# A hybrid diffusion backbone on one core: two buffers each for the pooling mixer's inputs and gates, and the modulation's gates stored as rows

## The chip, the cores and the metric

The kernel runs on one core of a Trainium2 chip. The metric is the device time of one execution in microseconds (us), lower is better. Five engines work side by side, each through its own queue in order: PE (TensorE, products; PEld is its weight load), DVE (VectorE), ACT (ScalarE), POOL (GpSimd) and SP (SyncE, which here only issues transfers). Transfers between the chip's DRAM and the on-chip memory run on 16 DMA engines; in this kernel SP issues the weight loads and POOL most others.

## The reference

Two layers work on 512 latent tokens and 256 context tokens, each 1024 wide. Cut to what matters:

```python
for l in range(DEPTH):                                  # DEPTH = 2
    mod   = silu(c)     @ mod_w[l] + mod_b[l]           # 3 x 1024: shift, scale, gate (latents)
    mod_c = silu(c_ctx) @ mod_w[l] + mod_b[l]           # the same for the context
    z, zc = (rmsnorm(x) * (1 + scale) + shift) @ w_in, ...     # one projection for all branches
    y_mla  = attention(...) * silu(z.mla_gate)          # 8 heads, keys of context and latents
    y_pool = (pooled @ pool_w) * pool_scale * silu(z.pool_gate)
    y_gla  = gated_linear_attention(...) * silu(z.gla_gate)
    merged = sum(sigmoid(z.merge_b) * (y_b @ w_branch_b) for b in (mla, pool, gla))
    x  = x  + gate   * rmsnorm(merged @ w_out)
    xc = xc + gate_c * rmsnorm(merged_c @ w_out)        # not in the last layer
```

In the pooling mixer, `pooled` is, for each of four groups of 128 channels, the mean over a window of 2, 4, 8 or 16 tokens minus the token itself.

## The kernel before

All tokens of a layer (768, or 512 where only latents count) lie along the free dimension, channels on the 128 partitions. Products are made in float32 as three products of split halves: each weight load `raw_...` is split by ACT (`wh_...`, line 77) and DVE (`wl_...`, line 78) before PE can use it (`mm3`, lines 91 to 94). What one stage leaves for a later one goes through DRAM.

The kernel is written for a planner. It traces the program once, and when the context closes it orders each engine's instructions by a simulation of the time line (line 1244); the order of the program is the priority, and `urgent` raises it. Buffers are named by tags: tiles of one tag share `bufs` slots, and a tile that takes a slot waits until all users of the slot's former tile are done.

A layer runs in this order: the gated linear attention (`gla_tile`, six token tiles), the projections of the gates and inputs that go to DRAM (`gate_block` for `gg`, `px`, `pg`, `mg`), the output of the linear attention, the **pooling mixer** (lines 689 to 736), the softmax attention (head by head), the 24 merge gates `m1`, `m2`, `m0` (`zA_m` in the profile), the three branch products (`br_p`, `br_g`, `br_m`), and the output product with the residual (`wo`). The planner lays the merge gates, which need only the layer's input, between the steps of the mixer and of the attention.

**The pooling mixer.** A loop over the four groups makes these steps: clear the padded input `u` (POOL, line 700), load it from DRAM (line 702), build the window sums `pn` (DVE, lines 705 to 715), the difference `pv` with its edges (lines 716 to 723), split it (`pvh`, `pvl`), load the gate `sg` (`psg` in the profile, line 728), apply tanh and the gate, multiply by the group's weights (`pps`), put both together in `sg` (line 735) and store it as `yp` (line 736). The mixer takes its buffers from tags that the linear attention used: `u` from `up0`, `sg` from `afab`, each one slot, so that all four groups use the same slot in turn. The tag `e` held the decays of the linear attention (1024 numbers per partition; `u` has 816 or 544), and `lmask` a table of masks (768 numbers; `sg` has 768).

**The modulation.** The 3072 outputs of a layer are made in 12 chunks of 256 (`modulation`, lines 155 to 255). `columns` (line 168) writes a chunk as two columns of `cols`, one channel per partition, for each of two streams (latents and context; one stream for the gates of the last layer). Chunks 8 to 11 are the gates: they are multiplied by the post norm and stored to `grow` in DRAM (lines 178 to 180), one DMA per chunk and stream. At the end of the layer `gate_rows` (line 259) loads each stream's 1024 gates from `grow`, spread over all partitions, as `pg`, which line 1056 and line 1072 multiply by. The chunks are made one after another by `chunk_beside_pe`, on DVE and POOL (`macc`) with a small product `modt` on PE, while the merge gates run: the generator `todo_mod` is advanced at line 913 and line 1000.

Of the kernel before, what the change touches and what calls it, by code (L numbers as in the profile page):

```python
# [11 lines left out]
F32 = mybir.dt.float32  # L12
# [6 lines left out]
P = 128  # L19
D = 1024  # L20
KD = 8
CTX = 256
LAT = 512
T = CTX + LAT
NT = T // P
DEPTH = 2
# [22 lines left out]
def hybrid_kernel(ctx, tc, io, out):  # L49
    nc = tc.nc  # L50
    V, S, G, PE = nc.vector, nc.scalar, nc.gpsimd, nc.tensor
# [8 lines left out]
    stage = ctx.enter_context(tc.tile_pool(name="stage", bufs=2))  # L60
    small = ctx.enter_context(tc.tile_pool(name="small", bufs=4))
    dram = ctx.enter_context(tc.tile_pool(name="dram", bufs=1, space=MemoryType.DRAM))
    psz = ctx.enter_context(tc.tile_pool(name="psz", bufs=2, space=MemoryType.PSUM))
# [3 lines left out]
    def act(out, in_, func=AF.Copy, **kw):  # L67
        return S.activation(out=out, in_=in_, func=func, **kw)  # L68

    def tt(out, a, b, op=ALU.mult, eng=None):  # L70
        return (eng or V).tensor_tensor(out=out, in0=a, in1=b, op=op)  # L71

    def stt(out, a, s, b, op0=ALU.mult, op1=ALU.mult):
        return V.scalar_tensor_tensor(out=out, in0=a, scalar=s, in1=b, op0=op0, op1=op1)  # L74
# [13 lines left out]
    def mm(out, lhsT, rhs, start, stop):  # L88
        PE.matmul(out=out, lhsT=lhsT, rhs=rhs, start=start, stop=stop)  # L89
# [14 lines left out]
    def load_raw(src, nk, width, name, pool=stream):  # L104
        raw = pool.tile([P, nk, width], F32, tag="raw", name=f"raw_{name}", bufs=3 if pool is stream else None)
        nc.sync.dma_start(out=raw, in_=src)
        return raw
# [17 lines left out]
    ident = const.tile([P, P], F32, name="ident")  # L125
# [29 lines left out]
    def modulation(l, pool=None):  # L155


        cols = const.tile([P, 24, 2], F32, tag=f"mcols{l}", name=f"mcols{l}")
        grow = dram.tile([2, D], F32, name=f"grow{l}")
        mods[l] = (cols, grow)  # L160
        modb = small.tile([P, 24], F32, tag="modb", name=f"modb{l}", bufs=1)
        nc.gpsimd.dma_start(out=modb, in_=io["mod_b"][l])
        pre = small.tile([P, KD], F32, tag="pre", name=f"pre{l}", bufs=1)
        nc.gpsimd.dma_start(out=pre, in_=io["pre_norm"][l])
        post = small.tile([P, KD], F32, tag="post", name=f"post{l}", bufs=1)
        nc.gpsimd.dma_start(out=post, in_=io["post_norm"][l])

        def columns(j, pt, streams=2):

            at = slice(2 * j, 2 * j + 2)  # L170
            dst = cols[:, at, 0:streams]

            def spread(v, c0):
                return v[:, 2 * j - c0:2 * j - c0 + 2].unsqueeze(2).to_broadcast([P, 2, streams])

            tt(dst, pt[:, :, 0:streams], spread(modb, 0), ALU.add)
            if j >= 8:
                tt(dst, dst, spread(post, 16))
                for st in range(streams):
                    nc.gpsimd.dma_start(out=grow[st].rearrange("(b p) -> p b", p=P)[:, 2 * j - 16:2 * j - 14], in_=dst[:, :, st])  # L180
            elif j >= 4:

                stt(dst, dst, 1.0, spread(pre, 8), ALU.add, ALU.mult)

        def chunk_on_pe(j):
            parts = j in (5, 6, 3, 7)
            ps = pst.tile([4 if parts else 2, 256], F32, tag="t", name=f"modps{l}_{j}")
            for half in range(2):
                raw = pool.tile([P, 4, 256], F32, tag="raw", name=f"raw_mod{l}_{j}_{half}", bufs=10)
                nc.sync.dma_start(out=raw, in_=io["mod_w"][l, j][:, 4 * half:4 * half + 4, :])  # L190
                if parts:
                    wh = pool.tile([P, 4, 256], F32R, tag="xin", name=f"mwh{l}_{j}_{half}", bufs=6)
                    wl = pool.tile([P, 4, 256], F32R, tag="xin", name=f"mwl{l}_{j}_{half}", bufs=6)
                    act(wh, raw)
                    tt(wl, raw, wh.bitcast(F32), ALU.subtract)
                for k in range(4):
                    kk = 4 * half + k
                    if parts:
                        mm(ps, chl[:, kk, :], wh[:, k, :], kk == 0, False)
                        mm(ps[0:2], chl[:, kk, 0:2], wl[:, k, :], False, kk == KD - 1)  # L200
                    else:
                        mm(ps, csil[:, kk, :], raw[:, k, :], kk == 0, kk == KD - 1)
            n = 4 if parts else 2
            row = pool.tile([n, 256], F32, tag="modrow", name=f"modrow{l}_{j}")
            act(row, ps)
            pt = psz.tile([P, 2, 2], F32, tag="z", name=f"modt{l}_{j}")
            for i in range(2):
                mm(pt[:, i], row[:, i * P:(i + 1) * P], sel[0:n], True, True)
            columns(j, pt)

        def chunk_beside_pe(j):

            streams = 2 if j < 8 or l < DEPTH - 1 else 1
            acc = small.tile([P, 2, 256], F32, tag="macc", name=f"macc{l}_{j}", bufs=1)
            for half in range(2):
                raw = load_raw(io["mod_w"][l, j][:, 4 * half:4 * half + 4, :], 4, 256, f"mod{l}_{j}_{half}")
                for k in range(4):
                    kk = 4 * half + k
                    for st in range(streams):
                        c = csil[:, kk, st:st + 1]  # L220
                        w, a = raw[:, k], acc[:, st]
                        eng = (G if streams == 1 and kk%2 else V) if st==0 else (G if kk%2 else V)
                        if kk == 0:
                            (eng if eng is G else V).tensor_scalar(out=a, in0=w, scalar1=c, scalar2=None, op0=ALU.mult)
                        elif eng is V:
                            stt(a, w, c, a, ALU.mult, ALU.add)
                        else:
                            if eng is S:
                                act(w, w, scale=c)
                            else:  # L230
                                G.tensor_scalar(out=w, in0=w, scalar1=c, scalar2=None, op0=ALU.mult)  # L231
                            tt(a, a, w, ALU.add, G)
            yield
            pt = psz.tile([P, 2, 2], F32, tag="z", name=f"modt{l}_{j}")
            for i in range(2):
                for st in range(streams):
                    mm(pt[:, i, st:st + 1], acc[:, st, i * P:(i + 1) * P], ones, True, True)
            columns(j, pt, streams)


        pend = []
        for j in (0, 4, 1, 5, 2, 6, 3, 7, 8, 9, 10, 11):
            if pool is not None and j < 8:
                chunk_on_pe(j)
            else:
                pend.append(chunk_beside_pe(j))
                next(pend[-1])
                if len(pend) > 1:
                    next(pend.pop(0), None)
            if j == 11 or (pool is None and j == 7):  # L250
                yield
                for chunk in pend:
                    next(chunk, None)
                pend = []
            yield

    mods = {}

    def gate_rows(l, pool, streams):

        grow = mods[l][1]
        res = []
        for s in range(streams):
            pgt = pool.tile([P, D], F32, tag=f"pg{s}", name=f"pg{l}_{s}", bufs=1)
            nc.gpsimd.dma_start(out=pgt, in_=grow[s].partition_broadcast(P))
            res.append(pgt)
        return res

# [81 lines left out]
    def layer(l, hT, close_hT, side, todo_mod):  # L350
# [64 lines left out]
        gl = g1.enter_context(opened(f"gla{l}", 2, side))  # L415
        psg = g1.enter_context(opened(f"psg{l}", 4, None, MemoryType.PSUM))
# [53 lines left out]
        afab = gl.tile([98, T], F32R, tag="afab", name=f"afab{l}", bufs=1)  # L470
# [11 lines left out]
        lmask = gl.tile([P, len(LEVELS), P], U32, tag="lmask", name=f"lmask{l}", bufs=1)  # L482
        nc.gpsimd.dma_start(out=lmask, in_=io["lmask"])

        f, b = slice(0, 64), slice(64, 128)
# [210 lines left out]
        segs = [(16, 0, CTX), (16 + CTX + 16, CTX, LAT)] if full else [(16, CTX, LAT)]  # L696
        W = segs[-1][0] + LAT + 16
        for g, w in enumerate(WINDOWS):
            u = gl.tile([P, W], F32, tag="up0", name=f"pu{l}_{g}", bufs=1)
            G.memset(u, 0.0)  # L700
            for s0, t0, n in segs:
                nc.gpsimd.dma_start(out=u[:, s0:s0 + n], in_=px_d[g][:, t0:t0 + n])
# [21 lines left out]
            pvh = gl.tile([P, T], F32R, tag="up1", name=f"pvh{l}_{g}", bufs=1)  # L724
            pvl = gl.tile([P, T], F32R, tag="dn1", name=f"pvl{l}_{g}", bufs=1)
            split(pvh[:, lo:T], pvl[:, lo:T], pv[:, lo:T])
            sg = gl.tile([P, T], F32, tag="afab", name=f"psg{l}_{g}", bufs=1)
            nc.gpsimd.dma_start(out=sg[:, lo:T], in_=sg_d["p"][g][:, lo:T])
            sig = gl.tile([P, T], F32, tag="pqk", name=f"psig{l}_{g}")
            half_tanh(sig[:, lo:T], sg[:, lo:T])  # L730
# [158 lines left out]
        for i in range(-AHEAD, len(units)):  # L889
            if i + AHEAD < len(units):  # L890
                u = units[i + AHEAD]
# [4 lines left out]
            if i >= 0:  # L896
                u = units[i]
# [358 lines left out]
```

## Time and profile before

| | |
|---|---|
| runs | 1512.39, 1515.74, 1519.95 us; median 1515.74 |
| the profiled execution | 1514.81 us, its span in the profile 1513.0 |
| PE | 1444.7 us busy, 95% of the span |
| DVE, ACT, POOL | 71%, 47%, 34% |
| mean granted clock of PE | 0.984 |
| DMA | 209.75 MB, mean 139 GB/s |

The rows of the profile name an engine, a line of the kernel, and the tiles written and read (out<-in). Where a helper issues an operation its line is the helper's: L89 is every product, L68 every activation, L71 and L74 the two tensor operations of DVE and POOL. In a timeline the first two numbers are the start and the length in us, and the brackets at the end give the idle time of that engine just before and what released it. In the chain of work that ended last, a row with DMA stands for the time from a transfer's issue to its landing. A row of the busy windows gives the stretch, its length, the busy us of PE, PEld, DVE, ACT and POOL with the count of instructions of each, the granted clock of PE, the mean busy share of the DMA engines and what they moved. That share is summed from the packets' own times, so it can pass 1.

### The profile page before, as it was taken

The page shows a single profiled execution, that of the slowest core. Times are in us where ns is not written, and L with a number is a line of the kernel's source. Part 1 is how long each engine was busy: PE and PEld are TensorE (multiplying, and loading weights), DVE is VectorE, ACT ScalarE, POOL GpSimd, SP SyncE. Part 2 cuts the span into 40 slices and gives each one's busy share as a digit, 9 for nine tenths or more (in the row PEclk, how much of TensorE's full clock was granted, in tenths as well). Part 3 has the DMA queues.
Part 4 walks back from the last instruction along what each step waited for, and adds up shares of the span by engine and source line. Part 5 has one row for each costly group of instructions (what it writes and reads, how often), then busy time and mean ns, then how long its engine had stood idle before and what let it go on. Part 6 is the DMA issues. An engine that isn't in the chain of part 4 may idle for free.

```text
span 1513.0 us, 23911 instructions
## 1 busy us (share of the span) xinstructions
PE 1444.7 (95%) x8940; PEld 1279.7 (85%) x8940; DVE 1066.7 (71%) x1980; ACT 717.3 (47%) x1340; POOL 521.8 (34%) x695
## 2 busy tenths in 40 slices
PE   7999999999997999997999999999999999998988
PEld 4799899998886889886879988988988888886778
DVE  3645999757576788876676373789976676686783
ACT  6554453343334445666443345654253555454532
POOL 3432333444243443542111064414463100053550
PEclk9999999999998999998999999999999999999999
DMA  9333323256544532346565234334356523157731
GB/s 366 108 125 113 107 96 115 90 166 192 183 74 101 144 118 90 130 147 163 173 210 198 82 126 129 124 127 127 100 180 204 164 96 96 51 151 145 232 132 69
DMA packets 64195, 209.75 MB, mean 139 GB/s; under 512 B 12464, under 2 KB 15696, under 8 KB 64080
## 3 DMA queue, kind: packets, MB, share of 16 engines
q1 hardware_dynamic: 38688, 116.74, 25.2%
q0 software_dynamic: 24528, 88.34, 18.3%
q10 hardware_dynamic: 864, 3.15, 0.5%
q8 instruction: 70, 1.15, 0.3%
q14 instruction: 45, 0.37, 0.1%
HBM read 161.65 MB, written 46.54 MB: 138 GB/s over the span
## 4 chain that ended last, share of the span: by engine, by line
PE 63%; issue 11%; DVE 11%; DMA 8%; POOL 3%; ACT 3%; POOLq 0%; DVEq 0%; SPq 0%; ACTq 0%
PE zA_m L89 13%; PE zB_gv L89 5%; PE zA_px L89 4%; PE zA_mg L89 4%; PE zB_wo L89 4%; PE wo L89 3%; DMA raw_m<-in_w_in 3%; PE lv L89 3%; PE zA_pg L89 3%; PE zA_gk L89 2%; PE br_p L89 2%; PE br_m L89 2%; PE br_g L89 2%; PE zB_qkv L89 2%; PE zA_gq L89 2%
## 5 line engine op out<-in xcount | busy, mean ns | idle before, releaser
L89 PE MATMUL zA_m<-hh,wh_m 128*128 128x512 f32 (+1 forms) x576 | 206.6, 359 | 1.0 <-ACT wh_m L68 1.0
L89 PE MATMUL zA_m<-hh,wl_m 128*128 128x512 f32 (+1 forms) x576 | 206.7, 359 | 0.6 <-DVE wl_m L71 0.6
L89 PE MATMUL zA_m<-hl,wh_m 128*128 128x512 f32 (+1 forms) x576 | 206.5, 359 | 0.0
L89 PEld LDWEIGHTS zA_m<-hh,wh_m 128*128 128x128 f32 x576 | 110.1, 191 | 16.0 <-ACT wh_m L68 1.4
L89 PEld LDWEIGHTS zA_m<-hh,wl_m 128*128 128x128 f32 x576 | 109.9, 191 | 15.6 <-DVE wl_m L71 1.1
L89 PEld LDWEIGHTS zA_m<-hl,wh_m 128*128 128x128 f32 x576 | 109.9, 191 | 14.4
L68 ACT ACTIVATE wh_m<-raw_m 128x1024 fp32r<-128x1024 f32 x48 | 50.9, 1060 | 93.0 <-PE zA_m L89 45.5
L68 ACT ACTIVATE pe<-sc,mx 128x768 f32<-128x768 f32 (+1 forms) x80 | 65.2, 814 | 60.2 <-DVE mx L831 59.7
L831 DVE TENSOR_REDUCE mx<-sc 128x1 f32<-128x768 f32 (+1 forms) x80 | 67.7, 846 | 34.7 <-PE sc L89 34.0
L71 DVE TENSOR_TENSOR wl_m<-raw_m,wh_m 128x1024 fp32r<-128x1024 f32 x48 | 59.0, 1228 | 45.6 <-ACT wh_m L68 45.1
L231 POOL TENSOR_SCALAR raw_mod<-raw_mod,csil 128x256 f32<-128x256 f32 x64 | 69.2, 1085 | 62.0 <-DVE macc L74 38.5
L74 DVE SCALAR_TENSOR_TENSOR macc<-raw_mod,csil,macc 128x256 f32<-128x256 f32 x132 | 70.8, 547 | 12.4 <-POOL macc L71 10.5
L68 ACT ACTIVATE pth<-pt 128x256 fp32r<-128x256 f32 (+1 forms) x144 | 61.8, 471 | 34.6 <-PE pt L853 34.0
L71 DVE TENSOR_TENSOR ptl<-pt,pth 128x256 fp32r<-128x256 f32 (+1 forms) x144 | 72.6, 534 | 7.2 <-ACT pth L68 6.2
L89 PEld LDWEIGHTS lv<-pqk 128*128 128x128 f32 x560 | 70.8, 191 | 4.7 <-issue 1.8
L347 POOL DMA_DIRECT2D sm<-st_m x32 | 17.6, 550 | 165.5 <-ACT st_m L68 148.1
L89 PE MATMUL lv<-pqk 128*128 128x128 f32 x560 | 73.4, 275 | 1.3 <-DVE pqk L71 1.2
L89 PE MATMUL sc<-kth,qth 96*128 96x256 f32 (+1 forms) x144 | 50.8, 353 | 19.0 <-ACT pe L68 18.9
L71 POOL TENSOR_TENSOR macc<-macc,raw_mod 128x256 f32<-128x256 f32 x64 | 55.1, 860 | 36.4 <-DVE macc L74 30.6
L89 PE MATMUL br_p<-yp,wh_wbp 128*128 128x512 f32 (+1 forms) x192 | 56.3, 376 | 8.6 <-ACT yp L68 6.8
L853 PE MATMUL pt<-ident,pe 128*128 128x128 f32 x416 | 61.3, 273 | 0.7 <-ACT pe L68 0.7
L89 PE MATMUL zB_gv<-wh_gv,hh 128*128 128x256 f32 x192 | 55.7, 291 | 4.1 <-ACT st_gv L68 2.1
(402 smaller groups left out, 4732.8 us busy)
## 6 DMA issues: line engine op xcount, KB each, us to landing
raw_mod<-in_mod_w SPq DMA_DIRECT2D x48, 512.0 KB, 5.0
raw_m<-in_w_in SPq DMA_DIRECT2D x48, 512.0 KB, 3.8
sm<-st_m POOLq DMA_DIRECT2D x24, 384.0 KB, 2.9
raw_wo<-in_w_out SPq DMA_DIRECT2D x16, 512.0 KB, 4.0
sm<-st_m POOLq DMA_DIRECT2D x24, 256.0 KB, 2.5
raw_gv<-in_w_gv SPq DMA_DIRECT2D x8, 512.0 KB, 4.6
raw_gg<-in_w_in SPq DMA_DIRECT2D x8, 512.0 KB, 4.0
raw_px<-in_w_in SPq DMA_DIRECT2D x8, 512.0 KB, 3.7
```

The lines of the kernel that those rows point to most:

```text
L68: return S.activation(out=out, in_=in_, func=func, **kw)
L71: return (eng or V).tensor_tensor(out=out, in0=a, in1=b, op=op)
L74: return V.scalar_tensor_tensor(out=out, in0=a, scalar=s, in1=b, op0=op0, op1=op1)
L89: PE.matmul(out=out, lhsT=lhsT, rhs=rhs, start=start, stop=stop)
L231: G.tensor_scalar(out=w, in0=w, scalar1=c, scalar2=None, op0=ALU.mult)
L347: nc.gpsimd.dma_start(out=dst[:, lo:T], in_=st[:, lo:T])
L831: V.tensor_reduce(out=mx, in_=ps[:, 0:nkey], axis=AX.X, op=ALU.max, negate=True)
L853: PE.transpose(out=pt[:, kk, :], in_=pe[:, (k0 + kk) * P:(k0 + kk + 1) * P], identity=ident)
```

## The change

Two edits are made together.

The pooling mixer's input `u` takes the tag `up0` in groups 0 and 2 and the tag `e` in groups 1 and 3. Its gate `sg` takes `afab` in groups 0 and 2 and `lmask` in groups 1 and 3. The sizes of these tags stay as they are.

The gates of the modulation are no longer stored chunk by chunk from their columns. When the last chunk (j = 11) of a layer is done, PE transposes the 16 gate columns (8 in the last layer) into rows of 128, ACT copies them from PSUM into a tile of the tag `st` (which the gate outputs use too, two slots), and one DMA stores the rows. `grow` changes its layout from (stream, channel) to (block of 128 channels, stream, channel in the block), and `gate_rows` loads it block by block.

```diff
@@ modulation
-        grow = dram.tile([2, D], F32, name=f"grow{l}")
+        grow = dram.tile([KD, 2 if l < DEPTH - 1 else 1, P], F32, name=f"grow{l}")
@@ columns
             if j >= 8:
                 tt(dst, dst, spread(post, 16))
-                for st in range(streams):
-                    nc.gpsimd.dma_start(out=grow[st].rearrange("(b p) -> p b", p=P)[:, 2 * j - 16:2 * j - 14], in_=dst[:, :, st])
@@ modulation, the loop over j
+            if j == 11:
+
+                n = KD * grow.shape[1]
+                pt = psz.tile([n, P], F32, tag="z", name=f"gateT{l}")
+                columns_ = cols[:, 16:24, :].rearrange("p b s -> p (b s)") if n > KD else cols[:, 16:24, 0]
+                PE.transpose(out=pt, in_=columns_, identity=ident)
+                row = stage.tile([P, P], F32, tag="st", name=f"gates{l}")
+                act(row[0:n], pt)
+                nc.gpsimd.dma_start(out=grow.rearrange("b s p -> (b s) p"), in_=row[0:n])
             yield
@@ gate_rows
-            nc.gpsimd.dma_start(out=pgt, in_=grow[s].partition_broadcast(P))
+            nc.gpsimd.dma_start(out=pgt.rearrange("q (b p) -> q b p", p=P), in_=grow[:, s].partition_broadcast(P))
@@ layer, the pooling mixer
-            u = gl.tile([P, W], F32, tag="up0", name=f"pu{l}_{g}", bufs=1)
+            u = gl.tile([P, W], F32, tag=("up0", "e")[g % 2], name=f"pu{l}_{g}", bufs=1)
...
-            sg = gl.tile([P, T], F32, tag="afab", name=f"psg{l}_{g}", bufs=1)
+            sg = gl.tile([P, T], F32, tag=("afab", "lmask")[g % 2], name=f"psg{l}_{g}", bufs=1)
```

## The prediction

> **What bounds the kernel now.** I read the busy table first, then the busy windows along the span, then at each gap of PE the timelines of PE, ACT, POOL and SP around it.
>
> ```profile
> PE 1444.7 (95%) x8940; PEld 1279.7 (85%) x8940; DVE 1066.7 (71%) x1980; ACT 717.3 (47%) x1340; POOL 521.8 (34%) x695
> ```
>
> PE has work for 1444.7 of 1513.0 us, so only its 68.3 us of idle time, and the time in which its clock is granted at half, can be won by moving things. Three gaps carry what this change can reach. The first, in layer 0 (timelines of POOL, SP, ACT and PE; start, length, engine, what):
>
> ```profile
> 443.70 1.48 POOL L180 DMA_DIRECT2D grow<-mcols  x2
> 444.53 16.19 DMA raw_m<-in_w_in
> 460.74 1.06 ACT L68 ACTIVATE wh_m<-raw_m 128x1024 fp32r<-128x1024 f32 x1 [13.88 <-DMA raw_m<-in_w_in]
> 461.82 0.90 ACT L68 ACTIVATE pe<-sc,mx 128x768 f32<-128x768 f32 x1
> 462.87 0.58 PE L89 MATMUL sc<-kth,qth 96*128 96x256 f32 x1 [10.22 <-ACT pe L68]
> ```
>
> Read it downward: POOL issues two stores of gate columns, a weight load (raw_m) issued 0.8 us later needs 16.19 us, ACT stands 13.88 us in its queue before the split of that weight, the softmax's exp behind it is late, and PE is idle for 10.22 us. The second and the third, at the start of the branches of layer 0 and in those of layer 1:
>
> ```profile
> 692.75 0.74 POOL L180 DMA_DIRECT2D grow<-mcols  x1 [0.32 <-DVE mcols L71]
> 695.17 10.41 DMA yrp<-yp
> 705.60 1.88 ACT L68 ACTIVATE yp<-yrp 128x512 fp32r<-128x512 f32 x4 [7.40 <-DMA yrp<-yp]
> 706.28 1.01 PE br_p L89 x2
> ...
> 1363.63 0.75 POOL L180 DMA_DIRECT2D grow<-mcols  x1
> 1364.82 0.33 SPq L106 DMA_DIRECT2D raw_wbp<-in_w_branch_p  x1
> raw_wbp<-in_w_branch_p SPq DMA_DIRECT2D x1, 512.0 KB, 11.2
> 1378.08 0.80 PE L89 MATMUL sc<-kth,qth 96*128 96x512 f32 x1 [4.75 <-ACT pe L68]
> ```
>
> The same figure each time: a store, behind it a late load, ACT held by it, PE idle. The list of DMA issues gives the usual landing times (last number, median us); the row of the gate stores' own view ends it, with the ns that one issue takes on POOL (least, median, most):
>
> ```profile
> raw_m<-in_w_in SPq DMA_DIRECT2D x48, 512.0 KB, 3.8
> raw_wbp<-in_w_branch_p SPq DMA_DIRECT2D x8, 512.0 KB, 4.5
> yrg<-yg SPq DMA_DIRECT2D x4, 384.0 KB, 3.4
> kn<-in_mla_kv_norm POOLq DMA_DIRECT2D x2, 0.5 KB, 3.5
> grow<-mcols POOLq DMA_DIRECT2D x12, 1.0 KB, 9.4
> L180 POOL DMA_DIRECT2D grow<-mcols x12: 716/742/776, 426.4 to 1387.1; - x12
> ```
>
> A store of 1 KB takes 9.4 us, over twice a load of 512 KB. It writes 256 single numbers (128 partitions, two columns each), 512 bytes apart in DRAM for the two columns and 4 bytes apart along the partitions. A load of 128 single numbers (kn) lands in 3.5, so single numbers alone don't explain it; their writes to DRAM may. Is it the store that holds the others up? In windows of 4 us (length, busy us of PE, PEld, DVE, ACT, POOL with counts, granted clock, DMA share, GB/s) I looked for a DMA share over 0.55 with under 75 GB/s, that is, engines occupied and moving little. There are nine in the span, these the first and the last:
>
> ```profile
> 444.00:448.00 4.00, 4.00 (x29) 3.70 (x28) 3.89 (x6) 1.55 (x5) 1.95 (x3) 1.00 1.14 33
> 1392.00:1396.00 4.00, 4.00 (x24) 3.38 (x23) 2.81 (x4) 1.75 (x4) 0.55 (x1) 1.00 0.83 46
> ```
>
> All nine begin within 10 us behind a gate store, and none elsewhere. The twelve stores stand at eight places (layer 0's four are pairs, one store for each stream; layer 1's four are single, the first of them already at 692.75); seven of the eight have such a window. That is why I hold the store for the cause.
>
> The clock is a second price of each gap:
>
> ```profile
> 462.00:466.00 4.00, 3.13 (x14) 3.13 (x15) 3.55 (x7) 2.03 (x4) 0.97 (x1) 0.50 0.36 124
> 466.00:470.00 4.00, 4.00 (x20) 3.37 (x19) 2.35 (x6) 0.84 (x3) 3.71 (x5) 0.95 0.27 105
> ...
> 704.00:708.00 4.00, 1.71 (x4) 1.18 (x5) 2.71 (x5) 2.34 (x6) 1.97 (x3) 0.50 0.70 228
> 708.00:712.00 4.00, 4.00 (x14) 3.32 (x13) 2.89 (x8) 3.49 (x8) 0.00 (x0) 0.50 0.89 296
> ...
> 1378.00:1382.00 4.00, 3.52 (x11) 3.06 (x12) 3.83 (x7) 3.81 (x8) 1.07 (x2) 0.50 0.45 136
> 1382.00:1386.00 4.00, 4.00 (x15) 3.19 (x14) 3.92 (x7) 2.19 (x4) 3.98 (x4) 0.67 0.76 209
> ```
>
> After each gap PE works at a clock of 0.50 for some us. Busy time times the missing share is lost: 3.13 x 0.50 + 4 x 0.05 = 1.8; 1.71 x 0.50 + 4 x 0.50 = 2.9; 3.52 x 0.50 + 4 x 0.33 = 3.1; together 7.8 us.
>
> **The change part by part.** *The gate store.* Twelve column stores go, and their 0.74 us each on POOL, which is idle two thirds of the time: worth nothing itself. What counts is the three gaps.
> - First gap: with raw_m landing in 3.8, at 448.3, the split (1.1) and the exp (0.9) would be done at 450.3, before PE ran dry (462.87 - 10.22 = 452.65). All 10.2 us go, and the 1.8 of clock.
> - Second: PE went on 0.7 us behind yrp's landing (695.17 + 10.41 = 705.58, then 706.28). With 3.4 us like yrg it lands at 698.6, and PE could go on at 699.3. One window of 1 us shows where it ran dry:
> ```profile
> 699.00:700.00 1.00, 0.45 (x5) 0.21 (x2) 0.00 (x0) 0.00 (x0) 0.00 (x0) 1.00 1.80 74
> ```
> That is 699.45, so the 6.8 us up to 706.28 go, and 2.9 of clock.
> - Third: raw_wbp, issued at 1364.8, would land at 1369.3, and split and exp would be done at 1371.3, ahead of PE's running dry at 1373.3: 4.75 us, and 3.1 of clock.
>
> Sum 10.2 + 6.8 + 4.75 + 7.8 = 29.6 us. What is late next? PE itself: behind each gap its windows are full, so it takes what it is given. In their place come, per layer, one transpose of 16 (8) columns, one ACT copy and one store of 16 (8) rows of 512 bytes.
>
> ```profile
> L89 PE MATMUL modt<-ones,macc x112: 164/250/352, 423.3 to 1380.7; 128*128 128x1 f32 x112
> L265 POOL DMA_DIRECT2D pg<-grow x3: 528/534/564, 816.9 to 1450.4; - x3
> L71 DVE TENSOR_TENSOR part<-part,pg x10: 684/692/693, 845.0 to 1485.9; 128x512 f32<-128x512 f32 x10
> osg<-sgg POOLq DMA_DIRECT2D x10, 256.0 KB, 3.5
> ```
>
> The transpose costs about a modt product, 0.25 us. It waits for DVE's last column sum and stands in PE's own queue: between nothing and the 10.22 us of the worst wait above plus 3.1 of clock, for each layer; I take 0.3, since modt makes the same turn from DVE for each of the 24 chunks and its view shows no idle time of PE before it. The ACT copy waits for one of the two st buffers, within the same bounds. Together 1 us. The gate rows are now read in pieces of 512 bytes in layer 0 instead of 4 KB: osg moves such pieces, 256 KB in 3.5 us, so 512 KB may take some 7. They are issued at 816.9 and first used at 845.0, so nothing is late; without that cover it would be those 7 us less what the load takes now.
>
> *The pool mixer.* The second gate load (L728) stops waiting for the store of the first product, and the input load (L702) for the readers of the former input.
>
> ```profile
> 358.02 0.62 POOL L728 DMA_DIRECT2D psg<-sgp  x1 [2.96 <-DMA yp<-psg]
> 350.00:416.00 66.00, 66.00 (x379) 58.02 (x378) 43.66 (x76) 24.23 (x38) 26.14 (x36) 1.00 0.60 193
> 1137.00:1205.00 68.00, 68.00 (x312) 56.24 (x311) 40.95 (x64) 30.51 (x49) 14.97 (x28) 1.00 0.58 190
> ```
>
> Per group 3 us for the store and about as long for the load leave the mixer's chain, for three groups up to 18 us per layer, and attention may begin that much earlier. But from the mixer's products to the first scores PE is busy without a break in both layers, with the merge gates (zA_m), which are due anyway. The cover is those 24 gate blocks; an earlier attention only shifts them behind it. I take 0, bounds -5 (a reorder that opens one gap like that at 540, below) and +5 (one such gap closed).
>
> Sum: 29.6 - 1.0 = 28.6 us off. The profiled execution took 1514.8 (span 1513.0 and 1.8 around it), 0.9 under the median of 1515.7; on the scale of the median 1515.7 - 28.6 = **1487**.
>
> **The rivals.** *The store isn't the cause.* The Trainium skill, "DMA: Bandwidth & Descriptors", Queues, rings and completion order, has each DMA engine take turns between queues packet by packet; by that rule a 1 KB store delays the loads of another queue by little, and its removal would win next to nothing. As a mechanism of this kernel: loads of SP and stores of POOL share the engines evenly, and the slow stretches come from something else. Against it stand nine of nine windows and loads at three times their usual landing. Time 1515. Chance 0.07.
>
> *Part of it comes back.* A planner that simulates the program sets the order of each engine's instructions at build time (line 1244), so the order comes out anew, and a split that moves ahead of its load in ACT's queue opens a gap without any store. One is there already:
>
> ```profile
> 540.00:544.00 4.00, 2.50 (x22) 2.06 (x20) 3.33 (x11) 2.11 (x5) 0.65 (x2) 1.00 0.66 229
> 544.00:548.00 4.00, 3.87 (x13) 3.19 (x14) 4.00 (x9) 1.11 (x4) 2.01 (x2) 0.62 0.36 122
> 548.00:552.00 4.00, 4.00 (x11) 3.09 (x11) 4.00 (x7) 1.94 (x3) 2.40 (x2) 0.53 0.03 11
> ```
>
> It costs 1.5 + 0.1 idle and 3.87 x 0.38 + 4 x 0.47 = 3.4 of clock, 5 us. Two or three new ones give 1497 to 1502. For: 48 gate blocks pass ACT's queue. Chance 0.22. The Trainium skill, "TensorE: Matmul & The Clock Gate", Part 1, says that the clock halves only after an idle window of about 3.4 us; by that page such a gap would cost its 1.6 us of idle time alone, and three of them would end at 1492. These rows show a half clock behind 1.5 us, so the page is not followed here.
>
> *Slower, by the same mechanism.* It decides from the eighth new gap: 8 x 5 = 40 against 28.6, 1527. Against: this trace has few gaps of the kind. Chance 0.05.
>
> *More than forecast.* The five other slow stretches, or an earlier attention, also free time: 4 to 13 us more, 1474 to 1483. Chance 0.10.
>
> **How the numbers follow.** Forecast 0.56 (1483 to 1494), back in part 0.22, more 0.10, nothing 0.07, slower 0.05. Range 1474 to 1505: it leaves out the last two and a little of the others. A measurement of this kernel can tell about 0.5% (7.6 us) from no change; faster than that is all but the last two, 0.88, same 0.07, slower 0.05.
>
> **What would show it.** Right: raw_m, yrp and raw_wbp land in under 6 us at these places, no window with high DMA share and little moved, no clock of 0.50 there, one gate store per layer, PE's busy time a few us lower (it is counted longer at half clock) and its idle time near 47; psg loads that wait for no yp store, with PE as full there as now. Wrong: the same late loads with no column store ahead (the first rival), or new ACT waits on loads elsewhere (the second).

## The result, and the profile after

The changed kernel takes 1491.5 us (median of five runs, 1487.9 to 1493.1) against 1515.7: 0.9835 of the time before, with a 95% interval from 0.9814 to 0.9857, or 24.2 us less. The forecast was 1487. The profiled execution took 1493.07 us, its span 1491.3, with a mean granted clock of 0.99 (0.984 before).

The busy table of the changed kernel's page:

```profile
PE 1440.8 (97%) x8942; PEld 1275.6 (86%) x8942; DVE 1065.7 (71%) x1980; ACT 717.6 (48%) x1342; POOL 516.3 (35%) x685
```

PE is busy for 3.9 us less, and idle for 1491.3 - 1440.8 = 50.5 us where it was 68.3. Its work is the same but for two transposes more. The clock's loss, added up in the table below, falls from 17.1 to 12.2 us, and a product takes longer at half clock: in the kernel before, one of br_p (128x512) takes 0.63 us at 709.8, in a window of clock 0.50, and 0.40 at 713.0, behind it. So the busy time that went is taken to be time at half clock.

The busy windows by stage: first the kernel before, from the first merge gate (zA_m) of layer 0 to its first branch product, from there to the output product (zB_wo), and the branches of layer 1:

```profile
349.00:693.00 344.00, 330.70 (x2057) 295.41 (x2056) 260.26 (x525) 164.82 (x343) 146.43 (x174) 0.98 0.45 131
693.00:822.00 129.00, 117.75 (x670) 101.73 (x669) 87.48 (x161) 60.89 (x104) 16.16 (x29) 0.96 0.58 178
1331.00:1456.00 125.00, 113.65 (x593) 94.29 (x591) 98.81 (x163) 62.18 (x116) 62.21 (x68) 0.97 0.66 176
```

and the same stages of the changed kernel:

```profile
351.00:685.00 334.00, 332.27 (x2085) 296.73 (x2084) 258.24 (x526) 169.97 (x355) 138.87 (x160) 0.99 0.40 131
685.00:798.00 113.00, 111.30 (x639) 95.13 (x638) 84.17 (x153) 53.84 (x91) 17.00 (x30) 1.00 0.63 205
1315.00:1436.00 121.00, 108.69 (x556) 91.38 (x554) 97.70 (x150) 61.55 (x110) 63.01 (x68) 0.95 0.59 191
```

Length less PE's busy time is PE's idle time: 13.3, 11.2 and 11.4 us before, 1.7, 1.7 and 12.3 after. The two stages of layer 0 are now filled. The branches of layer 1 are not: they are 4 us shorter, but only because fewer products lie in them (556 against 593); their idle time grew, and their clock fell from 0.97 to 0.95. All stages, with the clock's loss worked out from windows of 2 us as in the prediction (busy time by the share that is missing):

| stage | idle + clock loss before, us | after | difference |
|---|---|---|---|
| layer 0 up to the merge gates | 12.9 + 1.5 | 13.4 + 1.7 | +0.7 |
| layer 0, mixer and attention | 13.3 + 5.1 | 1.7 + 1.6 | -15.1 |
| layer 0, branches | 11.2 + 3.0 | 1.7 + 0 | -12.5 |
| layer 0 output, layer 1 up to the merge gates | 9.0 + 4.6 | 13.8 + 1.6 | +1.8 |
| layer 1, mixer and attention | 0 | 0 | 0 |
| layer 1, branches | 11.4 + 2.9 | 12.3 + 4.8 | +2.8 |
| layer 1, output | 10.5 + 0 | 7.3 + 2.5 | -0.7 |

The sum is -23.0; the spans of the two profiled executions differ by 21.7.

The places of the first two gaps, from the timelines of ACT and PE of the changed kernel:

```profile
472.83 1.06 ACT L68 ACTIVATE wh_m<-raw_m 128x1024 fp32r<-128x1024 f32 x1 [3.50 <-DMA raw_m<-in_w_in]
481.79 0.39 PE L89 MATMUL sc<-kth,qth 96*128 96x256 f32 x1 [0.78 <-ACT pe L68]
685.84 0.69 PE L89 MATMUL br_p<-yp,wh_wbp 128*128 128x512 f32 x2 [0.23 <-ACT yp L68]
690.77 0.94 ACT L68 ACTIVATE yp<-yrp 128x512 fp32r<-128x512 f32 x2 [0.95 <-DMA yrp<-yp]
```

ACT's wait for raw_m was 13.88 us and is 3.50, and PE's largest wait in that attention is 0.78 us instead of 10.22; at the first branch product it is 0.23. The transfers, from the list of DMA issues:

```profile
grow<-gates POOLq DMA_DIRECT2D x1, 8.0 KB, 4.1
pg<-grow POOLq DMA_DIRECT2D x3, 512.0 KB, 4.7
raw_m<-in_w_in SPq DMA_DIRECT2D x48, 512.0 KB, 4.0
```

The store of layer 0's 2048 gates lands in 4.1 us, less than half of what the store of 256 of them took. The 4.7 of pg is a median of three loads, of which only layer 0's two read in pieces of 512 bytes now: these land in 4.70 and 7.25 us, where they took 3.98 and 5.71 before. Over the whole span no window of 4 us has a DMA share above 0.55 with under 75 GB/s any more; there were nine.

In the branches of layer 1 there are other gaps now (timeline of PE):

```profile
1348.59 0.63 PE L860 MATMUL pt<-ident,pe 128*128 128x128 f32 x4 [1.54 <-DVE ptl L71]
1361.47 0.64 PE L860 MATMUL pt<-ident,pe 128*128 128x128 f32 x4 [1.36 <-ACT pe L68]
1372.68 0.38 PE L89 MATMUL av<-pth,vv 128*128 128x256 f32 x1 [1.71 <-ACT pth L68]
1436.38 0.55 PE L89 MATMUL zB_wo<-wh_wo,mh 128*128 128x256 f32 x1 [4.81 <-DVE gated L74]
```

The chain of waits names one transfer among them, a weight load that ACT waits for ahead of the third:

```profile
1365.58 5.49 DMA raw_wbg<-in_w_branch_g
```

The largest gap is at the stage's end, where PE waits for DVE; before, the largest wait of the output product was this (timeline of PE):

```profile
1463.94 0.38 PE L89 MATMUL zB_wo<-wh_wo,ml 128*128 128x256 f32 x1 [2.45 <-DVE ml L71]
```

The busy windows of the changed kernel at two of those gaps:

```profile
1368.00:1372.00 4.00, 2.98 (x15) 2.12 (x13) 1.89 (x2) 1.97 (x2) 0.19 (x1) 1.00 0.87 318
1372.00:1376.00 4.00, 2.54 (x8) 2.06 (x9) 4.00 (x7) 3.67 (x7) 1.11 (x2) 0.65 0.76 248
1376.00:1380.00 4.00, 4.00 (x17) 3.61 (x17) 2.24 (x5) 2.00 (x4) 1.56 (x2) 0.50 0.54 161
...
1431.00:1436.00 5.00, 0.57 (x3) 0.15 (x1) 5.00 (x6) 1.47 (x3) 2.35 (x2) 0.86 0.33 105
1436.00:1440.00 4.00, 3.62 (x17) 3.65 (x18) 4.00 (x7) 0.63 (x1) 0.78 (x1) 0.50 0.42 135
```

At 1368 the DMA engines move 318 GB/s, so this isn't the old way, with engines occupied and moving little. From 1431 to 1436 DVE is busy for all 5.00 us and PE for 0.57: the last gates and splits stand in DVE's queue. Both times the clock is at 0.50 afterwards.

The mixer did what its edit says. The first load behind it, of a norm of the attention, is issued at (first and last start at the row's end; before, then after):

```profile
L746 POOL DMA_DIRECT2D qn<-in_mla_q_norm x2: 540/541/542, 396.7 to 1170.4; - x2
```

```profile
L753 POOL DMA_DIRECT2D qn<-in_mla_q_norm x2: 542/550/558, 386.5 to 1135.9; - x2
```

Counted from the stage's start that is 47.7 us before and 35.5 after in layer 0 (396.7 - 349.0 and 386.5 - 351.0). The attention begins 12 us earlier, and PE was full there before as well.

### The profile page after: what moved, and what is told of

It reads as the page before. It is cut to its first block, busy times and chain, and to the rows that moved or that the text cites. A ratio compares the mean times of both kernels' runs of the same rounds, so it can differ in the third digit from the quotient of the medians.

```text
span 1491.3 us, 23912 instructions
## 1 busy us (share of the span) xinstructions
PE 1440.8 (97%) x8942; PEld 1275.6 (86%) x8942; DVE 1065.7 (71%) x1980; ACT 717.6 (48%) x1342; POOL 516.3 (35%) x685
## 4 chain that ended last, share of the span: by engine, by line
PE 75%; DVE 12%; issue 4%; DMA 3%; ACT 3%; POOL 3%; ACTq 0%; DVEq 0%; POOLq 0%
PE zA_m L89 20%; PE zB_gv L89 4%; PE sc L89 4%; PE zB_wo L89 4%; PE br_g L89 4%; PE br_m L89 3%; PE zA_pg L89 3%; PE zA_mg L89 3%; PE wo L89 3%; PE av L89 3%; PE br_p L89 3%; PE lv L89 2%; PE pt L860 2%; PE zA_px L89 2%; PE zA_gq L89 2%
## 5 line engine op out<-in xcount | busy, mean ns | idle before, releaser
L89 PEld LDWEIGHTS zA_m<-hh,wh_m 128*128 128x128 f32 x576 | 109.2, 190 | 14.7 <-ACT st_m L68 0.5
L89 PEld LDWEIGHTS zA_m<-hl,wh_m 128*128 128x128 f32 x576 | 109.2, 190 | 14.3
L89 PE MATMUL av<-pth,vv 128*128 128x256 f32 x208 | 55.3, 292 | 2.1 <-ACT pth L68 1.7
```

## Experiments

The theory: the column stores hold other queues' transfers up while they write, and that, not the mixer, is what the change wins. Its rivals: the mixer's buffers; the planner's new order; the store's being there at all, with its semaphore and its place in POOL's queue, rather than the way it writes. Each time is a median beside the kernel before on the same chip (1514.2 to 1515.3 us there); from ratios of different chips the differences are made on 1515 us. A spare store writes to a DRAM tile that nobody reads.

**Each half alone.** e1_rows_only is the changed kernel with the mixer's tags as before:

```diff
-            u = gl.tile(..., tag=("up0", "e")[g % 2], ...)
+            u = gl.tile(..., tag="up0", ...)
-            sg = gl.tile(..., tag=("afab", "lmask")[g % 2], ...)
+            sg = gl.tile(..., tag="afab", ...)
```

> The gates stored as rows, the pooling mixer with one buffer each as before. Theory A (the column stores hold the loads up, the mixer's buffers are worth about nothing): 1486 to 1498 us, about the time of the whole change, and no window of 4 us with a DMA share over 0.55 and under 75 GB/s. Theory B (the mixer's buffers, or the new order of the instructions, brought the gain): over 1508.

e2_mixer_only is the kernel before with these two edits made the other way round.

> The mixer's inputs and gates in two buffers each, the gates stored as columns as before. Theory A: 1508 to 1522 us, and behind nearly each of the eight places of column stores a window with high DMA share and little moved; PE idle near 68 us. Theory B: 1485 to 1500.

e1 took 1493.3 us, ratio 0.9853 [0.9827, 0.9879]; e2 1522.7, ratio 1.0052 [1.0034, 1.0071]. The rows alone give the gain: the whole change is 2.7 us below e1, well within the intervals. The mixer's buffers alone cost 8 us, just above what was expected of e2. In e2 the pattern of before is there, in new places (timeline of PE, then a busy window):

```profile
713.48 1.52 PE L89 MATMUL br_p<-yp,wh_wbp 128*128 128x512 f32 x3 [8.71 <-ACT yp L68]
```

```profile
704.00:708.00 4.00, 0.77 (x7) 0.53 (x5) 0.35 (x1) 0.00 (x0) 0.29 (x1) 0.91 0.77 28
```

It has five such windows where the kernel before had nine, and still lost more: PE is idle for 71.3 us, and the clock takes 20.6. Why just these 8 us was not settled; the kernels differ in order on every engine. One gap of the changed kernel is in e2 too, the one before the output product of layer 1 (timeline of PE):

```profile
1463.22 0.55 PE L89 MATMUL zB_wo<-wh_wo,mh 128*128 128x256 f32 x1 [4.65 <-DVE gated L74]
```

e1's longest wait there is 1.69 us, so the rows didn't bring this gap.

The windows of e1 at the place of the changed kernel's new gap in layer 1:

```profile
1368.00:1372.00 4.00, 4.00 (x21) 3.33 (x20) 3.61 (x6) 1.93 (x3) 0.78 (x3) 1.00 1.01 344
1372.00:1376.00 4.00, 4.00 (x23) 3.35 (x22) 3.89 (x6) 3.17 (x6) 2.08 (x4) 1.00 0.95 351
```

In another order there is no gap at this place; the branches of layer 1 take 114.6 us in e1 (first br_p to first zB_wo) and 120.9 in the changed kernel, with more of PE's work in them (busy 109.2 us against 108.2, none of it at half clock).

**The columns back, with everything else kept.** e3_rows_and_columns adds the twelve column stores to the whole change as spare stores:

```diff
+        spare = dram.tile([2, D], F32, name=f"spare{l}")
...
                 tt(dst, dst, spread(post, 16))
+                for st in range(streams):
+                    nc.gpsimd.dma_start(out=spare[st].rearrange("(b p) -> p b", p=P)[:, 2 * j - 16:2 * j - 14], in_=dst[:, :, st])
```

> The whole change, and beside it the twelve column stores of before, into a DRAM tile that nobody reads; nothing waits for their data. Theory A: 1505 to 1525 us, the slow windows are back behind the stores. Theory B: within 5 us of the whole change (1487 to 1497). If the time lies between, only some of the places hit loads that PE waits for.

1532.2 us, ratio 1.0116 [1.0091, 1.0141]: all of the gain is gone and 17.6 us more, 7 us above the upper end of what was expected. But here the order is new as well. e5_columns_apart writes the same numbers with the same stores, each number 512 bytes from the next in DRAM:

```diff
-        spare = dram.tile([2, D], F32, name=f"spare{l}")
+        spare = dram.tile([2, KD, P, P], F32, name=f"spare{l}")
...
-                    nc.gpsimd.dma_start(out=spare[st].rearrange("(b p) -> p b", p=P)[:, 2 * j - 16:2 * j - 14], in_=dst[:, :, st])
+                    nc.gpsimd.dma_start(out=spare[st, 2 * j - 16:2 * j - 14, :, 0].rearrange("b p -> p b"), in_=dst[:, :, st])
```

> The run with rows and columns, its twelve column stores with the same 256 numbers each, but each number written 512 bytes from the next in DRAM; every engine's instructions stand in the same order as there. If neighbouring 4-byte writes are what holds the loads up: 1488 to 1500 us, within 8 of the whole change, and no window of high DMA share with little moved. If it is the count of 4-byte pieces, or any small store from POOL at that place: 1520 to 1537, as with rows and columns.

1503.8 us, ratio 0.9925 [0.9906, 0.9944]. On each of the five engines e3 and e5 have the same instructions in the same order, so only where the 256 numbers land differs. That alone is 0.0191 of the time, 29 us (give or take 5). The spare stores' own view gives their landing (least, median, most), and the timeline of ACT its wait for yrp; e3 first:

```profile
DMA to landing us min/median/max: 7.1/9.2/10.6
```

```profile
713.19 0.94 ACT L68 ACTIVATE yp<-yrp 128x512 fp32r<-128x512 f32 x2 [9.51 <-DMA yrp<-yp]
```

and the same two of e5:

```profile
DMA to landing us min/median/max: 2.0/2.2/4.8
```

```profile
698.00 0.94 ACT L68 ACTIVATE yp<-yrp 128x512 fp32r<-128x512 f32 x2 [0.24 <-DMA yrp<-yp]
```

e3 has six windows of the occupied kind, e5 none. e5 is still 13.6 us above the whole change, more than was expected of it. By idle time and clock loss, 8 us of that are in the branches of layer 0 and some 3.5 each in the mixer and attention before them and in the stage behind. No transfer from 400 to 780 us takes longer than 7.2 us in it (7.3 in the changed kernel), and the order of the instructions is another on every engine; that the order costs the 13.6 us is the likely reading, and was not tested by itself.

**The transfers by themselves.** e4_transfers_alone loads two blocks of 512 KB by SP behind one small store, for eight kinds of store (none; col, as before; coltwo, a pair of them; far, 512 bytes apart; pair, 8 bytes per partition side by side; pairfar, 8 bytes each 512 bytes apart; rows; colsp, col issued by SP), five rounds of all eight.

```diff
+    for rnd in range(5):
+        for n, store in kinds.items():
...
+            store()
+            for x in xs:
+                k += 1
+                nc.sync.dma_start(out=x, in_=io["w_in"][0, k % 38])
```

> All computation is left out: two weight loads of 512 KB from SP, each time behind one small store, five rounds of: no store; the column store as before (256 numbers, 128 partitions, neighbours 4 bytes apart); two of them; 256 numbers each 512 bytes apart; 128 pieces of 8 bytes side by side; 128 pieces of 8 bytes 512 bytes apart; 16 rows of 512 bytes; the column store issued by SP. Theory A: the two loads behind no store or behind rows land in 4 to 7 us, behind the column store in 9 or more, and behind two of them later still. If neighbouring 4-byte writes are what is slow, the stores 512 bytes apart cost little; if the count of pieces is, they cost the same. Theory B: all within 1 us of no store.

The list of DMA issues (last number, median us to landing):

```profile
x<-in_w_in SPq DMA_DIRECT2D x82, 512.0 KB, 4.4
d_col<-c POOLq DMA_DIRECT2D x15, 1.0 KB, 9.4
d_far<-c POOLq DMA_DIRECT2D x5, 1.0 KB, 4.1
d_pair<-c POOLq DMA_DIRECT2D x5, 1.0 KB, 5.2
d_pairfar<-c POOLq DMA_DIRECT2D x5, 1.0 KB, 4.0
d_rows<-r POOLq DMA_DIRECT2D x5, 8.0 KB, 3.7
d_col<-c SPq DMA_DIRECT2D x5, 1.0 KB, 8.8
```

The chain of waits of the first round, one row for each kind, in the order none, col, coltwo, far, pair, pairfar, rows, colsp:

```profile
6.41 4.48 DMA x<-in_w_in
...
12.01 8.95 DMA x<-in_w_in
...
22.27 11.76 DMA d_col<-c
...
34.94 5.05 DMA x<-in_w_in
...
41.10 4.98 DMA x<-in_w_in
...
47.20 4.74 DMA x<-in_w_in
...
53.06 4.54 DMA x<-in_w_in
...
58.90 12.73 DMA x<-in_w_in
```

The rows of x are the second of the two loads. This load needs 4.48 us without a store, 8.95 behind a column store of another queue, and 12.73 behind one that SP itself issued. In the other rounds the chain behind col waits for 8.4 to 9.2 us each time, be it for the load or for the store itself. Behind the kinds that aren't columns it waits for 4.2 to 5.3 us, but for 6.3 once behind pair. The first load, which SP issues 0.1 us behind the store, is not held up when the store is POOL's. The list of DMA issues for these two moments of the first round, col, has them one by one:

```profile
x<-in_w_in SPq DMA_DIRECT2D x1, 512.0 KB, 3.3
x<-in_w_in SPq DMA_DIRECT2D x1, 512.0 KB, 8.9
```

In all five rounds it lands in 3.3 to 3.6 us, just as without a store, against 9 or more expected of both; the second, issued 0.4 to 0.8 us later, lands 0.4 to 0.5 us behind the store. Behind SP's own column store both are late (11.3 to 12.2 and 12.1 to 12.9). A stride of 512 bytes takes the effect away, and writing 8 neighbouring bytes per partition instead of two numbers in two places takes most of it. Whether the size of a piece or the number of pieces to 512 bytes decides is open.

**One layer at a time, and two numbers instead of 256.** e6_columns_layer0 and e7_columns_layer1 are e3 with the spare stores of one layer alone; e10 and e11 are these two with each store cut to one partition, two numbers:

```diff
-                for st in range(streams):
+                for st in range(streams if l == 0 else 0):
...
-[:, 2 * j - 16:2 * j - 14], in_=dst[:, :, st])
+[0:1, 2 * j - 16:2 * j - 14], in_=dst[0:1, :, st])
```

(the first edit in e6 and e10, with l == 1 in e7 and e11; the second in e10 and e11).

> The run with rows and columns, with the column stores of layer 0 alone (eight, in four pairs). By the terms of the prediction layer 0's stores cost 12 us (10.2 idle, 1.8 of clock): 1500 to 1508. If what the stores cost depends on which load happens to stand behind them, anything from 1492 to 1515.

> The same with the column stores of layer 1 alone (four single ones, the first at the start of layer 0's branches). By the terms of the prediction they cost 17.5 us (6.8 + 2.9 and 4.75 + 3.1): 1505 to 1514; by the run with rows and columns, which lost 41 us in all, up to 1520.

> The run with layer 0's column stores, each store cut to one partition (two numbers instead of 256). ACT and SP have the same order of instructions as there, the other engines nearly so, but nothing is left to hold a load up. If the 13 us that layer 0's column stores added are their writes: 1488 to 1494. If they are the new order that any added store brings: 1500 to 1506. The run with the columns apart, 13 us above the whole change, leaves both open.

> The same for layer 1's four column stores; PE, DVE, ACT and SP have exactly the order of the run with the full stores. By the writes: 1487 to 1493 (14 us less than with the full stores). By the order: 1501 to 1507.

The lengths of the stages hold PE's work as well, and the planner moves work between the stages; they are compared between e6 and e10 and between e7 and e11, where the order is held or nearly so.

| | us | ratio | layer 0: zA_m to br_p, br_p to zB_wo | layer 1: br_p to zB_wo |
|---|---|---|---|---|
| before | 1515.7 | 1 | 344.5, 128.0 | 125.0 |
| the change | 1491.5 | 0.9835 [0.9814, 0.9857] | 334.8, 112.2 | 120.9 |
| e6, layer 0 | 1503.0 | 0.9922 [0.9899, 0.9946] | 351.1, 113.0 | 114.4 |
| e10, two numbers | 1497.9 | 0.9893 [0.9871, 0.9916] | 344.3, 111.3 | 114.3 |
| e7, layer 1 | 1504.1 | 0.9931 [0.9906, 0.9955] | 333.0, 119.3 | 131.3 |
| e11, two numbers | 1485.9 | 0.9810 [0.9788, 0.9832] | 333.4, 112.2 | 117.9 |

e7 and e11 have the same order on PE, DVE, ACT and SP. The 254 numbers less in each of layer 1's four stores are worth 0.0121, 18 us (give or take 5; each of the two kernels is 1 us below the range expected of it); the prediction's second and third gap, both behind layer 1's stores, came to 9.7 + 7.85 = 17.55. It shows at the first store, which layer 1's gates send out while layer 0's branches begin. The chain of waits of e7:

```profile
686.13 9.88 DMA yrp<-yp
696.02 0.02 issue
696.04 0.64 ACT yp L68
```

This is the second of the loads of yrp. It and the third are issued between 684 and 688 us in both kernels; the list of DMA issues for this stretch, e7 first, then e11:

```profile
yrp<-yp SPq DMA_DIRECT2D x2, 384.0 KB, 10.2
yrp<-yp SPq DMA_DIRECT2D x2, 384.0 KB, 3.3
```

The same two loads take 10.2 us in the one and 3.3 in the other. Layer 0 is less clear: e10's time lies between the ranges of the two theories. e6 and e10 differ by 4.4 us and their intervals overlap; in the stage of the stores they differ by 6.8 us (351.1 and 344.3), with ACT and SP in the same order and the others nearly so.

**The change once more.** e8_whole_again is the changed kernel itself.

> The whole change once more, on the chip of these runs, as what they are compared with: 1488 to 1494 us by both theories.

1490.2 us, ratio 0.9836 [0.9814, 0.9859]. Its profile has the gap before zB_wo again (4.82 us), and this row (timeline of PE), which the first profile of the same kernel doesn't have:

```profile
1365.35 0.28 PE L258 MATMUL gateT<-ident,mcols 128*8 128x128 f32 x1 [1.88 <-DVE mcols L71]
```

e11 comes out 3.8 us below the change by its ratio (the intervals overlap), with four small stores more and nothing less to do; if there is a difference its order happens to suit, and it is no version of its own.

## Why the prediction was right, and where it was not

**The cause** was right, and is shown: with the order of every engine held, the way in which the columns are written is worth 29 us (e3 and e5), and the second of two loads is late behind the same store with nothing else in the program (e4). The first rival, loads and stores sharing the engines evenly, falls. The Trainium skill, "DMA: Bandwidth & Descriptors", Queues, rings and completion order, lets an engine take turns packet by packet; if that left a load almost untouched, as the prediction took it, e4's 4.48 against 8.95 us for the second load does not agree, and the first load's 3.3 does. The Trainium skill's same page says in Back-pressure in remote DMA that "Stalled writes stall the source SDMA engine's other queues too"; it says so of transfers between cores, and e4's rows look the same for writes to DRAM. Why the engines stay occupied is not shown.

**First and second gap.** Forecast 12.0 and 9.7 us, found 15.1 and 12.5 by the stage table, since other short waits of these stages went too. The landing times were right: yrp in 3.3 us without the full store (e11), raw_m in 4.0.

**Third gap: the step that failed.** The prediction gave it 4.75 + 3.1 = 7.85 us. The store's price in this stage was, if anything, larger: e7 less e11 is 13.4 us there, e3 less e5 15.6 (135.7 and 120.1). But the changed kernel has 2.8 us more of idle time and clock loss in this stage than the kernel before, not 7.85 less. The answer to "What is late next? PE itself" is what failed: late next are the softmax (1.54, 1.36 and 1.71 us) and, before zB_wo, DVE (4.81). That is the second rival, part comes back by the new order, in one stage only. Where the order is another, the third gap does pay: in e1, which has the rows, and in e6 and e10, which have rows and buffers and spare stores in layer 0 only, idle time and clock loss of this stage are 5.5, 7.6 and 6.8 us, against 14.3 before, so 7 to 9 less. Neither the rows nor the buffers as such bring the new gaps, then; what is left is the order, and which instruction moved was not followed up.

**New costs.** Forecast 0.3 us of PE's waiting per layer for the transposes. In the profile of the changed kernel PE waits for nothing before either transpose; in e8's, the same kernel, it waits for DVE's last column sum for 1.88 us in layer 1. So 0.3 was within what came, but the bound was better founded than the value. The gate loads in pieces of 512 bytes, put at some 7 us and hidden, land in 4.70 and 7.25, some 0.7 and 1.5 later than before.

**The mixer.** Taken as 0 within 5 us either way: 2.7 us better with the rows (e1 against the change), within the intervals. With the columns kept it was 8 us worse (e2), outside. The prediction's bound "a reorder that opens one gap" was too small for a program that still has slow stores in it. "psg loads that wait for no yp store" was wrong in detail: groups 2 and 3 take the slots of groups 0 and 1, and that wait remains.

**The sum.** 28.6 us forecast, 24.2 found: the two gaps of layer 0 gave 5.9 more than forecast, the third gave 10.7 less, and the rest is in the other stages. That the total came within 5 us is in part luck, since these two errors have opposite signs. PE's idle time, forecast near 47, is 50.5. The clock's rule from "TensorE: Matmul & The Clock Gate", Part 1, of the Trainium skill, a half clock only after about 3.4 us of idle time, was rightly not followed: the row at 1376 shows 0.50 behind waits of 1.71 us and less.

## What to carry to other kernels

Before a small store is put down as free, look at how its pieces lie in DRAM: many single numbers side by side took 9 us and held up loads issued shortly behind them, and a transpose in front of the store, or a stride between the numbers, ends that. A window with a high DMA share and little moved was the sign of it in these profiles. And where a planner sets the order anew, nearly the same work came out up to 14 us slower (e5 against the change), so a step of a few us is to be judged between kernels whose order is the same.

## What the runs showed of the hardware

A store of 1 KB in neighbouring pieces of 4 bytes (9.4 us) takes over twice as long as a load of 512 KB (4.4), and one of 8 KB in rows 3.7; the engine that issues it makes little difference to that (9.4 by POOL, 8.8 by SP). The same 256 pieces 512 bytes apart take 4.1 us, although they touch far more of the DRAM, and 128 pieces of 8 bytes side by side 5.2. A partition broadcast of 512 KB read in pieces of 512 bytes is little slower than one in pieces of 4 KB (4.70 and 7.25 us in the changed kernel's layer 0, 3.98 and 5.71 in the kernel before).
